# Second-product weight blocks read where they are summed, h2 kept in halves, and one group's order written out on two engines

## The chip, the cores and the metric

The kernel runs on one core of one Trainium2 chip. The metric is the device time of one execution in microseconds (us), as a median over runs. The profile is of one execution and has a time of its own.

## The reference

One encoder layer on 512 tokens of width 1024 in float32: a mixer with three branches (convolution, attention, spatial gating), then a feed-forward part. The change touches the feed-forward part alone:

```
h = rms_norm(x, norm_ffn_pre[l])                                   # 512 x 1024
f = jnp.square(jax.nn.relu(h @ w_ffn_up[l])) @ w_ffn_down[l]       # 1024 -> 4096 -> 1024
x = x + rms_norm(f, norm_ffn_post[l])
```

## The kernel before, in words

**Number format.** Every operand of a matrix product is cut into a high part (a copy on ACT into fp32r, `w_hi`, `h2h`) and a low part (original minus high on DVE, `w_lo`, `h2l`), and a product is three matmuls: high x high, high x low, low x high. So before PE can use a weight block of 128x1024, ACT makes one pass over it and DVE another behind it, and DVE's pass is needed by the third matmul.

**First product (h @ w_ffn_up).** The normalised `h`, transposed, lies in `h2h` and `h2l` (8 blocks of 128 rows of the contraction, times 512 tokens). The first four of the 32 column tiles are made plainly (`early`, `PLAIN`, one run for each half of the tokens). The other 28 come in seven groups `q = 1..7` of four tiles. A group is a 2x2 block product done with seven products instead of eight (`product(o, q, i, ...)`, i = 0..6), each of 24 matmuls of 256 columns. Its weight operands are the blocks `11`, `12`, `22`, the running sum `w_sum` (after 2, 3 and 4 additions) and `21 + 11`: `operand(q, i)` makes sum, high and low part. Its other operands are quarters of `h2` (products 0, 1 and 4) or four signed sums T[0..3] of the quarters (products 2, 3, 5, 6). These sums are the same for all groups and are made once, in `side()` and `parts()`, in the tiles `f` (scratch) and `ring`, at the start of group 1. Products 0 and 1 read the first and the second half of the contraction for the first 256 tokens, product 4 the second half for the others. The first half of `h2` is thus read last by product 0 of group 7, the second half by product 4 of group 7. Results leave through `snap` (a copy on ACT), `plus` (an addition on DVE) and `f_out` (two passes on ACT).

**Second product (f @ w_ffn_down).** The first half of the contraction is again done with seven block products p1, p5, p6, p2, p7, p4, p3 of four steps each (12 matmuls of 512 columns a step), the second half plainly in 16 steps (1, i) and (2, i) (24 matmuls a step), in the order of `seq`: p1 x4, (1,0), (1,1), p5 x2, (1,2), p5 x2, (1,3), p6 x2, (1,4), and so on. With B11, B12, B21, B22 the four blocks of the weights, p1 wants B11, p5 wants t1 = B11 + B12, p6 wants t1 + B22, p7 wants t3 = B22 + B12. Each of t1 and t3 comes in four pieces of 128x1024: a plain transfer from SP's queue brings B11 (or B22), and a transfer from POOL's queue with `accum_op=ALU.add` adds B12 to it in place. The pieces of t1 lie where `h2h` was and those of t3 where `h2l` was (same tags `hh`, `hl`). B11 for p1 and B22 for p6 are loaded a second time, like all other blocks, through three buffers `raw` (`top_up`). `prep(n + 2)` at step n makes the low and high parts of step n + 2 and of the moving operand of step n + 3.

**What sets the order.** TensorE's order is the program's (`keep_in_program_order`). On ACT, DVE, SP and POOL a scheduler places instructions when the kernel is built, by its own estimate of times; each engine then runs its row in order, and an instruction that waits holds everything behind it. A new tile in a tag waits until all readers of the old tile are done, as one whole.

Of the kernel before, what the change touches and what calls it, by code (L numbers as in the profile page):

```python
# [16 lines left out]
P = 128  # L17
# [31 lines left out]
def encoder_layer(ctx: ExitStack, tc: tile.TileContext, a: dict, out: bass.AP):  # L49
# [201 lines left out]
    def k_of(t):  # L251
        return t.rearrange("p (k s) -> p k s", s=S)

    hh = k_of(held("hh", "hh", F32R))
    hl = k_of(held("hl", "hl", F32R))
    with mk("p0") as p0:
# [512 lines left out]


    h2h = k_of(held("h2h", "hh", F32R, SHIFT))
    h2l = k_of(held("h2l", "hl", F32R, SHIFT))
    with mk("p4") as p4:
# [67 lines left out]
    def snap(src, t=None):  # L841
        if t is None:
            t = fp.tile([P, S], F32, tag="sn", bufs=4, name="snap")
        act.activation(t, src, AF.Copy)
        return t
# [5 lines left out]
    ring = fp.tile([P, 8 * 1024 + P], F32R, tag="ring", name="ring")  # L851

    def half(j, at):
        return ring[:, at + j * 1024:at + (j + 1) * 1024]

    def f_out(n, ts, src, sign):

        act.activation(src, src, AF.Relu, scale=sign)
        act.activation(f[:, n:n + 2, ts], src.rearrange("p (x t) -> p x t", x=2), AF.Square)


    for n in range(PLAIN):
        b = eb[n]
        run(unit_gen(b[:, 256:512], early[n], h2, slice(256, 512)))
        r = fp.tile([P, S], F32, tag="r", bufs=2, name="r")
        act.activation(r, b, AF.Relu)
        act.activation(f[:, n], r, AF.Square)

# [22 lines left out]
    def block(j, k):  # L891
        h_, l_ = quarter(j, (t1, t2)[k])
        vec.tensor_tensor(q4(B[j, k]), f32(h_), f32(l_), op=ALU.add)

    def parts(i):
        hi, lo = half(2 * i, SHIFT), half(2 * i + 1, SHIFT)
        act.activation(hi, sums[4 + i], AF.Copy)  # L897
        vec.tensor_tensor(lo, sums[4 + i], f32(hi), op=ALU.subtract)
        T[i] = q4(hi), q4(lo)

    def side():

        block(0, 0)
        block(0, 1)
        vec.tensor_tensor(sums[4], B[0, 0], B[0, 1], op=ALU.subtract)
        block(1, 1)
        vec.scalar_tensor_tensor(sums[5], sums[4], -1.0, B[1, 1], op0=ALU.mult, op1=ALU.subtract)
        block(1, 0)
        vec.scalar_tensor_tensor(sums[6], sums[5], -1.0, B[1, 0], op0=ALU.mult, op1=ALU.subtract)
        vec.tensor_tensor(sums[7], B[1, 1], B[0, 1], op=ALU.subtract)  # L910

    def operand(q, i):

        if q >= FT // 4:
            return
        g = lambda n: blocks[q, n]
        if i == 2:
            blocks[q, "x"] = wp.tile([P, 1024], F32, tag="raw", bufs=3, name="w_sum")
            vec.tensor_tensor(g("x"), g("21"), g("22"), op=ALU.add)
        if i == 3:  # L920
            vec.tensor_tensor(g("x"), g("x"), g("11"), op=ALU.add)
        if i == 4:
            vec.tensor_tensor(g("x"), g("x"), g("12"), op=ALU.add)
        if i == 6:
            vec.tensor_tensor(g("21"), g("21"), g("11"), op=ALU.add)
        raw = g(("11", "12", "x", "x", "x", "22", "21")[i])
        hi = wp.tile([P, 1024], F32R, tag="hi", bufs=3, name="w_hi")
        lo = wp.tile([P, 1024], F32R, tag="lo", bufs=3, name="w_lo")
        act.activation(hi, raw, AF.Copy)  # L929
        vec.tensor_tensor(lo, raw, f32(hi), op=ALU.subtract)  # L930
        blocks[q, i] = [t.rearrange("p (k c) -> p k c", c=256) for t in (hi, lo)]

    def product(o, q, i, m, first):
# [8 lines left out]
    def plus(ps_, t):  # L942
        r = fp.tile([P, S], F32, tag="r", bufs=2, name="r")
        vec.tensor_tensor(r, ps_, t, op=ALU.add)
        return r
# [18 lines left out]
    for p_ in ("p4", "p3"):  # L964
        for i in range(4):
# [20 lines left out]
    raws = []  # L986
    state2 = {}

# [5 lines left out]

    def load_t1():

        for n, tag in (("t1", "hh"), ("t3", "hl")):
            t = held(n, tag, F32)
            state2[n] = [t[:, i * 1024:(i + 1) * 1024] for i in range(4)]
# [38 lines left out]
    def w_prep(step):  # L1038
        p_, i = step
        top_up()  # L1040
        mine = [raws.pop(0) for _ in w_raws(step)]
        if p_ in ("p5", "p6", "p4"):
            src = state2["t1"][i]
            if mine:
                vec.tensor_tensor(src, src, mine[0], op=ALU.add)
        else:
            src = state2["t3"][i] if p_ == "p7" else mine[0]
        hi = wp.tile([P, 1024], F32R, tag="hi", bufs=3, name="w_hi")
        lo = wp.tile([P, 1024], F32R, tag="lo", bufs=3, name="w_lo")
        act.activation(hi, src, AF.Copy)  # L1050
        vec.tensor_tensor(lo, src, f32(hi), op=ALU.subtract)  # L1051
        wparts[step] = [t.rearrange("p (k c) -> p k c", c=512) for t in (hi, lo)]
        top_up()

    def prep(n):

        if n == 0:
            f_prep(seq[0])
        if n + 1 < len(seq):
            f_prep(seq[n + 1])  # L1060
        if n < len(seq):
            w_prep(seq[n])
        for m, at in (("t1", 0), ("t3", 8)):
            if at <= n < at + 4:
                load_sum(m, n - at)

    side()
    operand(1, 0)
    parts(0)
    operand(1, 1)  # L1070
    for q in range(1, FT // 4):
        c1, c2 = 4 * q, 4 * q + 2
        def ahead(i):
            if i + 2 < 7:
                operand(q, i + 2)
# [4 lines left out]
            if q == 1 and i in (0, 2, 3):  # L1080
                parts({0: 1, 2: 2, 3: 3}[i])

        ahead(0)
        ba = bank("a")
        product(ba, q, 0, quarter(0, t1), True)
        s1 = snap(ba)
        ahead(1)
        bd = bank("b")
        product(bd, q, 1, quarter(1, t1), True)
        f_out(c1, t1, plus(bd, s1), 1.0)  # L1090
# [5 lines left out]
        se = snap(be)  # L1096
        ahead(3)
        product(ba, q, 3, T[1], False)
        sv = snap(ba)
        load_block(q + 1, "22")  # L1100
# [7 lines left out]
        f_out(c1, t2, plus(be, sv), 1.0)  # L1108
        ahead(5)
# [38 lines left out]
    def finish(nh, t, xs=None):  # L1148
# [7 lines left out]
        act.activation(jk, src, AF.Square, accum_out=ss[:, t, nh:nh + 1])  # L1156
        vec.tensor_tensor(us[:, t, hf], src, gpo[:, hf], op=ALU.mult)
        if nh == 0:
# [85 lines left out]
```

## Time and profile before

| | us |
|---|---|
| median of 3 runs (1073.16 to 1078.03) | 1076.43 |
| profiled execution, its own time | 1074.35 |
| its span in the profile | 1072.6 |
| around the span | 1.75 |

The profile lists for each engine how long it was busy, in 40 slices how fast TensorE's clock was (9 is full), and the chain of work that ended last. A row of the timeline reads: start, duration, engine, line, operation, what is written from what, how many, and in brackets how long the engine had been idle and what released it. Starts are counted from the span's beginning.

### The profile page before, as it was taken

The page shows a single profiled execution, that of the slowest core. Times are in us where ns is not written, and L with a number is a line of the kernel's source. Part 1 is how long each engine was busy: PE and PEld are TensorE (multiplying, and loading weights), DVE is VectorE, ACT ScalarE, POOL GpSimd, SP SyncE. Part 2 cuts the span into 40 slices and gives each one's busy share as a digit, 9 for nine tenths or more (in the row PEclk, how much of TensorE's full clock was granted, in tenths as well). Part 3 has the DMA queues.
Part 4 walks back from the last instruction along what each step waited for, and adds up shares of the span by engine and source line. Part 5 has one row for each costly group of instructions (what it writes and reads, how often), then busy time and mean ns, then how long its engine had stood idle before and what let it go on. Part 6 is the DMA issues. An engine that isn't in the chain of part 4 may idle for free.

```text
span 1072.6 us, 14742 instructions
## 1 busy us (share of the span) xinstructions
PE 1049.0 (98%) x5688; PEld 903.6 (84%) x5688; DVE 827.0 (77%) x1296; ACT 579.9 (54%) x902; POOL 23.7 (2%) x40
## 2 busy tenths in 40 slices
PE   8999999999999999999999999999999998899997
PEld 7989898988878888888888888889899997688885
DVE  6696878978997797998898455478888787667746
ACT  5456677776664742344222673354677775455641
POOL 3000000000000000000000000000000002100000
PEclk9999999999999999999999999999999999999999
DMA  7342332233233333322333233645334219834432
GB/s 223 83 137 61 97 96 82 79 84 94 79 99 98 99 101 97 97 79 82 95 98 98 79 88 100 232 130 172 104 99 135 84 60 274 236 97 139 164 130 79
DMA packets 140550, 122.35 MB, mean 114 GB/s; under 512 B 4277, under 2 KB 116961, under 8 KB 140480
## 3 DMA queue, kind: packets, MB, share of 16 engines
q1 hardware_dynamic: 135296, 108.02, 32.8%
q0 software_dynamic: 4464, 11.82, 4.4%
q10 hardware_dynamic: 720, 1.57, 0.4%
q8 instruction: 44, 0.72, 0.3%
q14 instruction: 26, 0.21, 0.1%
HBM read 113.01 MB, written 4.19 MB: 109 GB/s over the span
## 4 chain that ended last, share of the span: by engine, by line
PE 87%; DVE 5%; DMA 4%; ACT 3%; issue 1%; SPq 0%; DVEq 0%; ACTq 0%
PE ps_a L58 66%; PE ps_b L58 18%; PE ps_b L62 3%; DMA w_raw<-in_w_ffn_down_dram 3%; DMA w_raw<-in_w_in_dram 1%; DVE us L1164 0%; DVE w_lo L1051 0%; ACT y L738 0%; ACT ring L897 0%; DVE jk L814 0%; DVE w_lo L151 0%; PE ps_a L62 0%; ACT jk L812 0%; SPq L274 0%; ACT w_hi L150 0%
## 5 line engine op out<-in xcount | busy, mean ns | idle before, releaser
L150 ACT ACTIVATE w_hi<-w_raw 128x1024 fp32r<-128x1024 f32 x116 | 122.8, 1059 | 214.2 <-PE ps_a L58 177.1
L58 PE MATMUL ps_a<-hh,w_hi 128*128 128x512 f32 (+1 forms) x536 | 205.4, 385 | 0.0
L58 PE MATMUL ps_a<-hh,w_lo 128*128 128x512 f32 (+1 forms) x536 | 202.9, 381 | 0.0
L58 PE MATMUL ps_a<-hl,w_hi 128*128 128x512 f32 (+1 forms) x536 | 202.5, 380 | 0.0
L359 DVE SCALAR_TENSOR_TENSOR acc<-apad,convw,acc 128x512 f32<-128x512 f32 x232 | 173.7, 749 | 5.0
L151 DVE TENSOR_TENSOR w_lo<-w_raw,w_hi 128x1024 fp32r<-128x1024 f32 x116 | 141.6, 1221 | 41.5 <-ACT w_hi L150 41.2
L58 PEld LDWEIGHTS ps_a<-hh,w_lo 128*128 128x128 f32 x536 | 100.3, 188 | 19.6
L58 PEld LDWEIGHTS ps_a<-hh,w_hi 128*128 128x128 f32 x536 | 100.5, 188 | 18.3
L58 PEld LDWEIGHTS ps_a<-hl,w_hi 128*128 128x128 f32 x536 | 100.5, 188 | 18.3
L58 PE MATMUL ps_a<-ring,w_hi 128*128 128x256 f32 x336 | 59.6, 281 | 0.1
L58 PEld LDWEIGHTS ps_a<-ring,w_hi 128*128 128x128 f32 x336 | 51.9, 192 | 0.3 <-ACT w_hi L929 0.3
L58 PE MATMUL ps_a<-w_hi,hh 128*128 128x256 f32 (+1 forms) x160 | 49.7, 311 | 0.0
L58 PE MATMUL ps_a<-ring,w_lo 128*128 128x256 f32 x168 | 47.4, 282 | 2.2 <-DVE w_lo L930 2.2
L58 PE MATMUL ps_a<-h2h,w_hi 128*128 128x256 f32 x176 | 48.9, 278 | 0.0
L58 PE MATMUL ps_a<-h2l,w_hi 128*128 128x256 f32 x176 | 48.8, 277 | 0.0
L58 PE MATMUL ps_a<-h2h,w_lo 128*128 128x256 f32 x176 | 48.7, 277 | 0.0
L58 PE MATMUL ps_a<-w_hi,hl 128*128 128x256 f32 (+1 forms) x160 | 48.7, 304 | 0.0
L58 PE MATMUL ps_a<-w_lo,hh 128*128 128x256 f32 (+1 forms) x160 | 48.6, 304 | 0.0
L494 ACT ACTIVATE e<-ps_b,m 128x512 f32<-128x512 f32 x64 | 43.4, 682 | 7.3 <-DVE m L490 7.1
L1051 DVE TENSOR_TENSOR w_lo<-w_raw,w_hi 128x1024 fp32r<-128x1024 f32 x28 | 34.2, 1221 | 16.4 <-ACT w_hi L1050 16.4
L58 PE MATMUL ps_a<-w_hi,ring 128*128 128x512 f32 x144 | 45.4, 389 | 0.0
L490 DVE CUSTOM_DVE_ANT_0 ps_b<-ps_b,al 128x512 f32<-128x512 f32 x64 | 43.5, 699 | 0.6 <-PE ps_b L58 0.2
(306 smaller groups left out, 2438.4 us busy)
## 6 DMA issues: line engine op xcount, KB each, us to landing
w_raw<-in_w_in_dram SPq DMA_DIRECT2D x80, 512.0 KB, 3.7
w_raw<-in_w_ffn_down_dram SPq DMA_DIRECT2D x36, 512.0 KB, 4.1
w_raw<-in_w_ffn_up_dram SPq DMA_DIRECT2D x32, 512.0 KB, 4.7
w_raw<-in_w_proj_attn_dram SPq DMA_DIRECT2D x8, 512.0 KB, 3.9
w_raw<-in_w_proj_sgu_dram SPq DMA_DIRECT2D x8, 512.0 KB, 4.0
w_raw<-in_w_proj_conv_dram SPq DMA_DIRECT2D x8, 512.0 KB, 4.0
w_raw<-in_w_out_dram SPq DMA_DIRECT2D x8, 512.0 KB, 3.6
t<-in_w_ffn_down_dram SPq DMA_DIRECT2D x8, 512.0 KB, 11.0
```

The source lines that it names most:

```text
L58: return tc.keep_in_program_order(nc.tensor.matmul(*args, **kw))
L62: return tc.keep_in_program_order(nc.tensor.transpose(*args, **kw))
L150: act.activation(hi, raw, AF.Copy)
L151: vec.tensor_tensor(lo, raw, f32(hi[:, :]), op=ALU.subtract)
L359: vec.scalar_tensor_tensor(o, apad[:, c, j:j + S], convw[:, c, j:j + 1], acc, op0=ALU.mult, op1=ALU.add)
L490: vec.tensor_tensor_reduce(b, b, nal[:, 384 - q * P:896 - q * P], 1.0, 3.0e38, ALU.add, ALU.min, m)
L494: act.activation(e, b, AF.Exp, bias=m, scale=-1.0, accum_out=l)
L1051: vec.tensor_tensor(lo, src, f32(hi), op=ALU.subtract)
```

## The change

1. `h2h` and `h2l` become two tiles each, one for each half of the contraction (`held` gives a pair, `KOf` picks the half). The tags are `hha`, `hhb`, `hla`, `hlb`.
2. The plain transfers for t1 and t3 stand apart from the adding ones (`load_sum`, `add_sum`). The program issues the first two pieces of t1 after product 0 of group 7, the others after product 4. The adding transfers are issued in `prep` of p1 (for t1) and of p6 (for t3).
3. p1 takes its B11 from the piece of t1 before the addition, and p6 its B22 from the piece of t3 before the addition. The eight loads of these blocks into `raw` go.
4. In group 1, and in the four plain tiles ahead of it, the order on ACT and DVE is written out by hand and kept (`order`, `pin`): `plain`, `side`, `side_hi`, `side_lo`, `w_sum`, `w_hi`, `w_lo`, `first`. The pin ends with `pin[0] = False` after product 4 of group 1.
5. `us` and `xs` at the end become pairs of tiles too, and `xs` is loaded in two transfers.

```diff
-    def held(name, tag, dt, at=0):
-        return hp.tile([P, KT * S + P], dt, tag=tag, name=name)[:, at:at + KT * S]
+    def held(name, tag, dt, at=(0, 16)):
+
+        return [hp.tile([P, KT // 2 * S + n], dt, tag=tag + h_, name=name)[:, o:o + KT // 2 * S]
+                for h_, n, o in zip("ab", (112, 16), at)]
...
+    def order(i):
+
+        return tc.keep_in_program_order(i) if pin[0] else i
...
-    B_OF = {"p1": [(1, 1)], "p2": [(2, 1)], "p3": [(2, 2)], "p4": [(2, 1)], "p5": [], "p6": [(2, 2)],
-            "p7": []}
+    B_OF = {"p1": [], "p2": [(2, 1)], "p3": [(2, 2)], "p4": [(2, 1)], "p5": [], "p6": [], "p7": []}
...
     def load_sum(n, i):
-        t = state2[n][i].rearrange("p (k c) -> p k c", c=512)
-        k, c = (2 * i, 0) if n == "t1" else (8 + 2 * i, 512)
-        nc.sync.dma_start(t, rows("w_ffn_down", k, c))
-        pool.dma_start(t, rows("w_ffn_down", 2 * i, 512), accum_op=ALU.add)
+
+        if i % 2 == 0:
+            sums2[n, i // 2] = hp.tile([P, KT // 2 * S + (16 if i else 112)], F32,
+                                       tag=("hh" if n == "t1" else "hl") + "ab"[i // 2], name=n)
+        nc.sync.dma_start(sum_at(n, i).rearrange("p (k c) -> p k c", c=512),
+                          rows("w_ffn_down", *((2 * i, 0) if n == "t1" else (8 + 2 * i, 512))))
+
+    def add_sum(n, i):
+
+        pool.dma_start(sum_at(n, i).rearrange("p (k c) -> p k c", c=512), rows("w_ffn_down", 2 * i, 512),
+                       accum_op=ALU.add)
...
-        if p_ in ("p5", "p6", "p4"):
-            src = state2["t1"][i]
-            if mine:
-                vec.tensor_tensor(src, src, mine[0], op=ALU.add)
+        if p_ in ("p1", "p5", "p6", "p4"):
+            src = sum_at("t1", i)
+            if p_ in ("p6", "p4"):
+                vec.tensor_tensor(src, src, mine[0] if mine else sum_at("t3", i), op=ALU.add)
...
-        for m, at in (("t1", 0), ("t3", 8)):
-            if at <= n < at + 4:
-                load_sum(m, n - at)
-
-    side()
-    operand(1, 0)
-    parts(0)
-    operand(1, 1)
+        if n < len(seq) and seq[n][0] in ("p1", "p6"):
+            add_sum("t1" if seq[n][0] == "p1" else "t3", seq[n][1])
+
+
+    block(0, 0)
+    block(0, 1)
+    side(0)
...
+    def first(i):
+
+        if i == 0:
+            w_hi(1, 3)
+            w_lo(1, 3)
+            side_hi(2)
+            w_sum(1, 4)
...
+        elif i == 4:
+            w_lo(1, 6)
+            pin[0] = False
...
         product(ba, q, 0, quarter(0, t1), True)
+        if q == FT // 4 - 1:
+            for i in range(2):
+                load_sum("t1", i)
...
         if q == FT // 4 - 1:
-            top_up()
-            load_t1()
+            for n, i in (("t1", 2), ("t1", 3), ("t3", 0), ("t3", 1), ("t3", 2), ("t3", 3)):
+                if i == 0:
+                    top_up()
+                load_sum(n, i)
```

**DVE in group 1.** This is DVE's row from the low part of product 2's weights to the low part of product 3's (each `w_lo` is the low part of the next product's weights; `ring` is a low part of one of T[0..3], `w_sum` an addition into the running sum, `w_raw<-w_raw` the sum 21 + 11 for product 6, `r<-ps_b` is `plus`). Before:

```order
L930 TENSOR_TENSOR w_lo_6923<-w_sum_6920,w_hi_6922 128x1024
L944 TENSOR_TENSOR r_6985<-ps_b_6960,snap_6953 128x512
L921 TENSOR_TENSOR w_sum_6920<-w_sum_6920,w_raw_6783 128x1024
L898 TENSOR_TENSOR ring_6793<-f_6782,ring_6793 128x1024
L925 TENSOR_TENSOR w_raw_6785<-w_raw_6785,w_raw_6783 128x1024
L930 TENSOR_TENSOR w_lo_6957<-w_sum_6920,w_hi_6956 128x1024
```

And of the change, on to the low part for product 4 (`w_lo_6991`):

```order
L951 TENSOR_TENSOR w_lo_6925<-w_sum_6897,w_hi_6924 128x1024
L939 TENSOR_TENSOR w_sum_6897<-w_sum_6897,w_raw_6787 128x1024
L951 TENSOR_TENSOR w_lo_6960<-w_sum_6897,w_hi_6959 128x1024
L939 TENSOR_TENSOR w_sum_6897<-w_sum_6897,w_raw_6793 128x1024
L970 TENSOR_TENSOR r_6993<-ps_b_6965,snap_6957 128x512
L930 TENSOR_TENSOR ring_6797<-f_6786,ring_6797 128x1024
L951 TENSOR_TENSOR w_lo_6991<-w_sum_6897,w_hi_6990 128x1024
```

One pass instead of four stands between the low parts for products 2 and 3; the others moved behind.

**DVE in group 2.** The place is ahead of the low part for product 4 of group 2 (`w_lo_7232` before, `w_lo_7236` in the change), from the `plus` of product 1 on. `w_sum_7400` and `w_sum_7404` are the next group's running sum, `w_raw_7237` and `w_raw_7241` the next group's 21 + 11. Before:

```order
L944 TENSOR_TENSOR r_7226<-ps_b_7201,snap_7194 128x512
L923 TENSOR_TENSOR w_sum_7163<-w_sum_7163,w_raw_7061 128x1024
L919 TENSOR_TENSOR w_sum_7400<-w_raw_7237,w_raw_7296 128x1024
L930 TENSOR_TENSOR w_lo_7232<-w_sum_7163,w_hi_7231 128x1024
L925 TENSOR_TENSOR w_raw_7237<-w_raw_7237,w_raw_7235 128x1024
```

And of the change (`w_lo_7202` is the low part for product 3):

```order
L941 TENSOR_TENSOR w_raw_6999<-w_raw_6999,w_raw_6997 128x1024
L939 TENSOR_TENSOR w_sum_7167<-w_sum_7167,w_raw_6997 128x1024
L970 TENSOR_TENSOR r_7230<-ps_b_7205,snap_7198 128x512
L951 TENSOR_TENSOR w_lo_7202<-w_sum_7167,w_hi_7201 128x1024
L939 TENSOR_TENSOR w_sum_7167<-w_sum_7167,w_raw_7069 128x1024
L937 TENSOR_TENSOR w_sum_7404<-w_raw_7241,w_raw_7300 128x1024
L941 TENSOR_TENSOR w_raw_7241<-w_raw_7241,w_raw_7239 128x1024
L951 TENSOR_TENSOR w_lo_7236<-w_sum_7167,w_hi_7235 128x1024
```

The low part for product 3 moved behind the `plus`, and the next group's 21 + 11 moved ahead of the low part for product 4.

**SP's queue at the start of the second product.** `w_raw` are loads through the three buffers, t1 and t3 the plain transfers of the sums. Before:

```order
L992 DMA w_raw_8506<-in_w_ffn_down_dram 128x2x512
L992 DMA w_raw_8508<-in_w_ffn_down_dram 128x2x512
L992 DMA w_raw_8510<-in_w_ffn_down_dram 128x2x512
L1004 DMA t3_8513<-in_w_ffn_down_dram 128x2x512
L1004 DMA t1_8512<-in_w_ffn_down_dram 128x2x512
L992 DMA w_raw_8528<-in_w_ffn_down_dram 128x2x512
L1004 DMA t1_8512<-in_w_ffn_down_dram 128x2x512
L992 DMA w_raw_8565<-in_w_ffn_down_dram 128x2x512
L1004 DMA t1_8512<-in_w_ffn_down_dram 128x2x512
L992 DMA w_raw_8614<-in_w_ffn_down_dram 128x2x512
```

And of the change (t1_8383 and t3_8522 lie in the first halves, t1_8513 and t3_8525 in the second):

```order
L1016 DMA w_raw_8516<-in_w_ffn_down_dram 128x2x512
L1031 DMA t3_8522<-in_w_ffn_down_dram 128x2x512
L1031 DMA t1_8383<-in_w_ffn_down_dram 128x2x512 x2
L1031 DMA t3_8522<-in_w_ffn_down_dram 128x2x512
L1016 DMA w_raw_8518<-in_w_ffn_down_dram 128x2x512
L1016 DMA w_raw_8520<-in_w_ffn_down_dram 128x2x512
L1031 DMA t3_8525<-in_w_ffn_down_dram 128x2x512
L1031 DMA t1_8513<-in_w_ffn_down_dram 128x2x512 x2
L1031 DMA t3_8525<-in_w_ffn_down_dram 128x2x512
L1016 DMA w_raw_8660<-in_w_ffn_down_dram 128x2x512
```

Four transfers for the sums moved ahead of the second load through the buffers, and all eight now stand ahead of the fourth; the three first loads were B11 for p1 and are now the weights of (1,0), (1,1) and (1,2).

## Rows read from the trace of the kernel before

**Rows 1.** The page: busy time, share of the span and instructions of each engine; then the shares of the chain that ended last.

```profile
PE 1049.0 (98%) x5688; PEld 903.6 (84%) x5688; DVE 827.0 (77%) x1296; ACT 579.9 (54%) x902; POOL 23.7 (2%) x40
PE 87%; DVE 5%; DMA 4%; ACT 3%; issue 1%; SPq 0%; DVEq 0%; ACTq 0%
```

**Rows 2.** Waits of PE between 738 and 1066 us: who was waited for, total us, times, longest us.

```profile
PE ps_b L58 <- DVE w_lo L1051: 4.6, 3, 2.6
PE ps_a L58 <- DVE w_lo L930: 2.2, 2, 1.8
PE ps_a L58 <- ACT snap L844: 1.4, 1, 1.4
PE ps_b L58 <- ACT w_hi L1050: 1.4, 1, 1.4
```

**Rows 3.** Timeline of PE in group 1: the first matmul of product 1, the two that waited in products 2 and 3, the first of product 5.

```profile
754.71 0.28 PE L58 MATMUL ps_b<-h2h,w_hi 128*128 128x256 f32 x1
...
758.30 0.39 PE L58 MATMUL ps_a<-ring,w_lo 128*128 128x256 f32 x1 [0.49 <-DVE w_lo L930]
...
763.44 0.51 PE L58 MATMUL ps_a<-ring,w_lo 128*128 128x256 f32 x1 [1.75 <-DVE w_lo L930]
...
770.38 0.28 PE L58 MATMUL ps_b<-ring,w_hi 128*128 128x256 f32 x1
```

**Rows 4.** The chain that ended last, in order of time: product 1 of group 2 (start, us, what).

```profile
778.70 2.72 PE ps_b L58 x24
```

**Rows 5.** Stretches: us, busy time (and instructions) of PE, PEld, DVE, ACT, POOL, granted TensorE clock as a share of full, DMA share, GB/s.

```profile
763.40:767.00 3.60, 3.56 (x17) 3.56 (x18) 3.54 (x4) 2.00 (x2) 0.00 (x0) 0.53 0.44 145
788.00:885.00 97.00, 97.00 (x858) 97.00 (x858) 80.22 (x78) 72.67 (x101) 0.00 (x0) 1.00 0.31 98
885.00:930.00 45.00, 37.62 (x171) 30.20 (x170) 30.45 (x29) 22.71 (x28) 9.56 (x8) 0.92 1.01 274
...
924.00:927.00 3.00, 3.00 (x9) 2.32 (x8) 1.28 (x2) 0.00 (x0) 0.96 (x1) 0.50 1.12 229
```

**Rows 6.** Timeline of DVE in group 1: the first sums of `h2`, the first addition into `w_sum` (21 + 22), then everything from the low part of product 2's weights to that of product 3's.

```profile
739.97 3.49 DVE L893 TENSOR_TENSOR f<-h2h,h2l 128x1024 f32<-128x1024 f32 x3
...
752.46 1.22 DVE L919 TENSOR_TENSOR w_sum<-w_raw 128x1024 f32<-128x1024 f32 x1
...
757.02 1.23 DVE L930 TENSOR_TENSOR w_lo<-w_sum,w_hi 128x1024 fp32r<-128x1024 f32 x1 [1.08 <-ACT w_hi L929]
758.16 0.68 DVE L944 TENSOR_TENSOR r<-ps_b,snap 128x512 f32<-128x512 f32 x1
758.77 1.22 DVE L921 TENSOR_TENSOR w_sum<-w_sum,w_raw 128x1024 f32<-128x1024 f32 x1
759.90 1.22 DVE L898 TENSOR_TENSOR ring<-f,ring 128x1024 fp32r<-128x1024 f32 x1
761.03 1.22 DVE L925 TENSOR_TENSOR w_raw<-w_raw 128x1024 f32<-128x1024 f32 x1
762.17 1.22 DVE L930 TENSOR_TENSOR w_lo<-w_sum,w_hi 128x1024 fp32r<-128x1024 f32 x1
```

**Rows 7.** Timeline of ACT in group 1: the first pass on the first plain tile, and the high part of product 2's weights.

```profile
744.02 0.60 ACT L866 ACTIVATE r<-ps_a 128x512 f32<-128x512 f32 x1 [4.80 <-PE ps_a L58]
...
755.92 1.06 ACT L929 ACTIVATE w_hi<-w_sum 128x1024 fp32r<-128x1024 f32 x1
```

**Rows 8.** Timeline of PE in the second product: its first matmul, two that waited, and its last.

```profile
890.06 0.39 PE L58 MATMUL ps_a<-w_hi,ring 128*128 128x512 f32 x1
...
903.74 0.79 PE L58 MATMUL ps_b<-w_lo,f_part 128*128 128x512 f32 x1 [0.75 <-DVE w_lo L1051]
...
923.41 0.50 PE L58 MATMUL ps_b<-w_lo,ring 128*128 128x512 f32 x1 [2.62 <-DVE w_lo L1051]
...
1064.95 0.39 PE L58 MATMUL ps_a<-w_hi,f_part 128*128 128x512 f32 x1
```

**Rows 9.** The chain that ended last, in order of time: one step on which PE gets no rest, and the longest piece that is not PE's (from issue to landing).

```profile
893.90 12.87 DMA w_raw<-in_w_ffn_down_dram
...
1021.82 8.16 PE ps_b L58 x36
```

**Rows 10.** Issues at the start of the second product: SP's queue (L992 is a load through the buffers, L1004 a plain transfer of a sum, here t3's first piece), POOL's first adding transfer (which waits for that piece's landing); then the time from issue to landing of the transfers of the sums.

```profile
862.51 0.37 SPq L992 DMA_DIRECT2D w_raw<-in_w_ffn_down_dram  x1
...
881.59 0.37 SPq L992 DMA_DIRECT2D w_raw<-in_w_ffn_down_dram  x1
884.70 0.37 SPq L1004 DMA_DIRECT2D t<-in_w_ffn_down_dram  x1
...
889.08 1.22 POOL L1005 DMA_DIRECT2D t<-in_w_ffn_down_dram  x1 [150.59 <-DMA t<-in_w_ffn_down_dram]
...
DMA to landing us min/median/max: 3.8/9.9/13.7
```

**Rows 11.** DMA queues between 855 and 1000 us: packets, MB, share of the 16 engines' time. q1 is SP's, q0 POOL's (the eight adding transfers).

```profile
q1 hardware_dynamic: 9520, 18.35, 36.9%
q0 software_dynamic: 2176, 4.19, 15.9%
```

**Rows 12.** Timeline of DVE and ACT at the start of the second product: low part of p1's first weight block, high parts of its third and fourth.

```profile
886.92 1.22 DVE L1051 TENSOR_TENSOR w_lo<-w_raw,w_hi 128x1024 fp32r<-128x1024 f32 x1
...
891.40 1.04 ACT L1050 ACTIVATE w_hi<-w_raw 128x1024 fp32r<-128x1024 f32 x1
...
894.43 1.05 ACT L1050 ACTIVATE w_hi<-w_raw 128x1024 fp32r<-128x1024 f32 x1
```

More of the change, by code (lines that the diff above doesn't have):

```diff
@@ L843, in snap @@
             t = fp.tile([P, S], F32, tag="sn", bufs=4, name="snap")
-        act.activation(t, src, AF.Copy)
+        order(act.activation(t, src, AF.Copy))
         return t
@@ L892, in block, with side, side_hi, side_lo @@
         h_, l_ = quarter(j, (t1, t2)[k])
[L893 to L915, printed above, removed]
+        order(vec.tensor_tensor(q4(B[j, k]), f32(h_), f32(l_), op=ALU.add))
+    def side(i):
+        if i in (0, 3):
+            m, n = ((0, 0), (0, 1)) if i == 0 else ((1, 1), (0, 1))
+            order(vec.tensor_tensor(sums[4 + i], B[m], B[n], op=ALU.subtract))
+        else:
+            order(vec.scalar_tensor_tensor(sums[4 + i], sums[3 + i], -1.0, B[1, 2 - i], op0=ALU.mult,
+                                           op1=ALU.subtract))
+    def side_hi(i):
+        T[i] = q4(half(2 * i, SHIFT)), q4(half(2 * i + 1, SHIFT))
+        order(act.activation(half(2 * i, SHIFT), sums[4 + i], AF.Copy))
+    def side_lo(i):
+        order(vec.tensor_tensor(half(2 * i + 1, SHIFT), sums[4 + i], f32(half(2 * i, SHIFT)), op=ALU.subtract))
+    def w_sum(q, i):
         g = lambda n: blocks[q, n]
@@ L918, in operand, with w_hi, w_lo @@
             blocks[q, "x"] = wp.tile([P, 1024], F32, tag="raw", bufs=3, name="w_sum")
[L919 to L926, printed above, removed]
+            order(vec.tensor_tensor(g("x"), g("21"), g("22"), op=ALU.add))
+        elif i in (3, 4):
+            order(vec.tensor_tensor(g("x"), g("x"), g("11" if i == 3 else "12"), op=ALU.add))
+        elif i == 6:
+            order(vec.tensor_tensor(g("21"), g("21"), g("11"), op=ALU.add))
+    def w_hi(q, i):
         hi = wp.tile([P, 1024], F32R, tag="hi", bufs=3, name="w_hi")
         lo = wp.tile([P, 1024], F32R, tag="lo", bufs=3, name="w_lo")
-        act.activation(hi, raw, AF.Copy)
-        vec.tensor_tensor(lo, raw, f32(hi), op=ALU.subtract)
+        blocks[q, i] = hi, lo, blocks[q, ("11", "12", "x", "x", "x", "22", "21")[i]]
+        order(act.activation(hi, blocks[q, i][2], AF.Copy))
+    def w_lo(q, i):
+        hi, lo, raw = blocks[q, i]
+        order(vec.tensor_tensor(lo, raw, f32(hi[:, :]), op=ALU.subtract))
         blocks[q, i] = [t.rearrange("p (k c) -> p k c", c=256) for t in (hi, lo)]
+    def operand(q, i):
+        w_sum(q, i)
+        w_hi(q, i)
+        w_lo(q, i)
     def product(o, q, i, m, first):
@@ L1062, in prep @@
             w_prep(seq[n])
-        for m, at in (("t1", 0), ("t3", 8)):
-            if at <= n < at + 4:
-                load_sum(m, n - at)
-    side()
-    operand(1, 0)
-    parts(0)
-    operand(1, 1)
+        if n < len(seq) and seq[n][0] in ("p1", "p6"):
[3 more added lines that the diff above has]
+    side(0)
+    block(1, 1)
+    side(1)
+    block(1, 0)
+    plain(0)
+    plain_out(0)
+    side_hi(0)
+    side_lo(0)
+    plain(1)
+    w_hi(1, 0)
+    plain_out(1)
+    w_lo(1, 0)
+    side(2)
+    plain(2)
+    w_hi(1, 1)
+    plain_out(2)
+    side_hi(1)
+    w_lo(1, 1)
+    w_sum(1, 2)
+    side_lo(1)
+    plain(3)
+    w_hi(1, 2)
+    plain_out(3)
+    w_lo(1, 2)
+    w_sum(1, 3)
+    def first(i):
[4 more added lines that the diff above has]
+            w_sum(1, 4)
+        elif i == 1:
+            w_hi(1, 4)
+        elif i == 2:
+            side_lo(2)
+            w_lo(1, 4)
+            side(3)
+            w_hi(1, 5)
+            w_lo(1, 5)
+            w_sum(1, 6)
+            side_hi(3)
+            side_lo(3)
+        elif i == 3:
+            w_hi(1, 6)
+        elif i == 4:
+            w_lo(1, 6)
+            pin[0] = False
     for q in range(1, FT // 4):
@@ L1079, in ahead, with behind @@
                 prep(i - 5)
-            if q == 1 and i in (0, 2, 3):
-                parts({0: 1, 2: 2, 3: 3}[i])
+        def behind(i):
+            if q == 1:
+                first(i)
         ahead(0)
@@ L1089, in encoder_layer @@
         product(bd, q, 1, quarter(1, t1), True)
+        behind(1)
         f_out(c1, t1, plus(bd, s1), 1.0)
@@ L1096, in encoder_layer @@
         se = snap(be)
+        behind(2)
         ahead(3)
@@ L1099, in encoder_layer @@
         sv = snap(ba)
+        behind(3)
         load_block(q + 1, "22")
```

63 lines of the change are left out of this document (38 added, 25 removed).

## The prediction

> **What bounds the kernel now.** The first view is the page. PE is busy 98% of the span and holds 87% of the chain that ended last; what is left on that chain is DVE 5%, DMA 4%, ACT 3% [rows 1]. So PE is the bound, and an edit gains only where PE stops or runs slowly and something else ends that. The second view is the list of PE's waits over the part that the change touches: low parts of weights, L930 in the first product and L1051 in the second, and one `snap` and one `w_hi` beside them [rows 2]. A wait understates its cost, so I measured each place against PE's own pace.
>
> *Group 1.* Without rest a product takes 2.72 us [rows 4]. Product 1 starts at 754.71, so product 5 is due at 754.71 + 4 x 2.72 = 765.59; it starts at 770.38 [rows 3]. Loss: 4.8 us. Two waits of 0.49 and 1.75 for L930 lie in it [rows 3], and behind the second the granted clock is 0.53 for 3.60 us (between the chip's levels of 2.4 and 1.2 GHz) [rows 5], which is 3.60 x 0.47 = 1.7 us more. DVE shows why: after the low part for product 2 it does `plus`, an addition into `w_sum`, a `ring` pass and 21 + 11, and only at 762.17 the low part for product 3 [rows 6], which ends at 763.39. Product 3 was due at 754.71 + 2 x 2.72 = 760.15, its third matmul 0.23 later.
>
> *Start of the second product.* Its 720 matmuls (28 steps of 12, 16 of 24) at 8.16 / 36 = 0.227 us [rows 9] take 163.2 us. From 890.06 the end is due at 1053.3; the last starts at 1064.95 [rows 8] and ends 0.23 later. Loss: 11.9 us. The waits are at 903.74 and 923.41 [rows 8]; behind them the chain holds a load of 12.87 us [rows 9], and the DMA share from 885 to 930 is 1.01 [rows 5]. Clock 0.50 from 924 to 927 [rows 5] is part of the loss. So here the transfers are the limit: from 788 to 885 the share was 0.31 with the clock at 1.00 [rows 5].
>
> **The change, part by part.**
>
> *Transfers.* SP's queue moved 18.35 MB in 36.9% of 145 us, 35 loads of 524 KB: 145 x 0.369 / 35 = 1.53 us of all 16 engines each. The eight adding transfers took 15.9%: 2.88 us each [rows 11]. Eight loads go. Four plain transfers move ahead: they wait for the first half of `h2` alone, free after product 0 of group 7, four products before the second half. The second half comes free where t3's first piece is issued now, at 884.70 [rows 10], so the first at 884.7 - 4 x 2.72 = 873.8, where the share is 0.31. From 885 to 930 go four plain transfers and p1's fourth block (7.7 us) and as many of p6's four loads (6.1) as fall there: 45 x 1.01 = 45.5 us of transfers become 32 to 38, and the queue is no longer full. The three loads issued up to 881.59 [rows 10] were p1's and are now those of (1,0), (1,1), (1,2).
>
> *What is late next there.* (a) t1's second half, behind t3's third piece on SP. That piece would land like today's first, 884.70 to 889.08 [rows 10]; each next 1.53 later: t1's third at 890.6, fourth at 892.1. ACT makes the high parts of p1's third and fourth block at 891.40 and 894.43 today [rows 12]. No stall. (b) The adding transfers. The first may start after p1's first low part, 886.92 + 1.22 = 888.1 [rows 12]. With the longest landing of 13.7 [rows 10] it is in at 902. p5 begins after four p1 steps and two plain ones, at 890.06 + 10.9 + 10.9 = 911.8, its copies (1.05 + 1.22) at 909.5. Spare: 7 us. (c) Of t3, the addition comes after p6's DVE pass and p7 wants it only after the four steps of p2 and two plain ones at least, 21.8 us: hidden. I take the whole 11.9; the low end is 7.8 (third rival).
>
> *The pinned order.* I walk DVE's new row from its first pass, 739.97, with 1.14 from pass to pass, 1.22 to the end of one, 0.61 for a `plus` [rows 6], 1.25 where a pass needs the one before it, and 1.06 for ACT's `w_hi` [rows 7]. First, eleven passes: three of `block` and `side` up to s1 at 744.74, then 745.88 block, 747.01 low of T0, 748.14 low for product 0, 749.28 s2, 750.41 low for 1, 751.55 first `w_sum`, 752.68 low of T1. Then low for 2 at 753.88, ends 755.10 (due 757.65, the third matmul); `w_sum` 755.13; `w_hi` to 757.43; low for 3 to 758.68 (due 760.37, 1.7 spare where 3.0 was lacking); `w_sum` 758.71; `plus`; T2's low; low for 4 to 762.80 (due 763.09); s3; low for 5 to 765.07 (due 765.81); 21 + 11; T3's low; `plus`; low for 6 to 769.07 (due 768.53): 0.5 to 0.6 late. So of 4.8 in group 1 about 0.6 stays.
>
> *Behind the pin.* The scheduler's row for group 2 is another: 21 + 11 of the next group stands ahead of the low part for product 4, and the low part for 3 behind `plus`. From 769.07 the same walk gives: low for 3 at 778.2 to 779.4 (due 780.0), then three additions at 779.4, 780.6 and 781.8, then low for 4 at 783.0 to 784.2. Group 2 starts at 771.6, product 4's third matmul is due at 771.6 + 4 x 2.72 + 0.23 = 782.7: 1.5 late. Left: 0.6 + 1.5 = 2.1; gain 4.8 - 2.1 = 2.7. Bounds: 4.8 if neither is late, 0 by the fourth rival.
>
> *Nothing for the rest.* The halves read the same elements with the same instructions. The order of groups 3 to 7 is as before. `xs` in two transfers adds one on POOL, busy 2% [rows 1].
>
> **Sum.** 11.9 + 2.7 = 14.6, bounds 7.8 and 16.7. All of it lies inside the span of 1072.6, and the 1.75 around it stays, so the profiled execution's 1074.35 gives 1059.75. The median of the runs shown is 2.08 above it; I carry half of that: **1060.8**.
>
> **Rivals.** What can be told from no change in this kernel is 0.5%, 5.4 us: 1071.05 to 1081.8.
>
> 1. *DVE becomes the bound at the second product's start.* It is busy 30.45 of 45 us there, and its best share over a long stretch is 80.22 / 97 = 0.827 [rows 5]. The same work at that share takes 36.8 us; PE without stops wants 45 - 11.9 = 33.1. Then 3.7 less is gained: 1064.5. Against it, DVE's passes stand back to back in [rows 6], so the share can be higher.
>
> 2. *The halves come free no earlier* (the change doesn't do what it says): all transfers at 884.7. p1's blocks then land from 889 on, the first some 1 late against today's 890.06, the others by 4 to 5, and the clock falls once (1.7): some 6.8 less, 1067.6. Against it, product 0 of group 7 is the last reader of the first half.
>
> 3. *t1's last piece shares the engines with the first adding transfer.* If it lands as the load on the chain did, 12.87 [rows 9] after an issue at about 885.7, that is 898.6, with copies 900.9, against p1's fourth step's third matmul at 890.06 + 3 x 2.72 + 0.23 = 898.45: 2.4 late, and 1.7 of clock. 4.1 less: 1064.9. For it, the loads landed in 4.4 to 12.9 here [rows 9, 10]; against it, that was under a full queue. The Trainium skill, DMA: Bandwidth & Descriptors, section Queues, rings and completion order, says that a DMA engine takes turns between the queues it has work for, packet by packet, so an adding transfer issued later does push back a load already on its way. By that rule one adding transfer (2.88) would move the landing from 892.1 to 895.0 and cost nothing, two to 897.9 and cost 1.7 before the clock; a 12.87 beside two busy queues agrees with it.
>
> 4. *Group 1 gives back all.* The first addition into `w_sum` moves from 752.46 [rows 6] to 751.55. The trace shows no wait there, so block 22 may have landed any time before. If it lands at 752.46, all behind shifts by 0.9: low for 4 is 0.6 late, for 6 1.5 late, and the clock falls (1.7); with the 1.5 in group 2 nothing of the 4.8 is left: 1060.8 + 2.7 = 1063.5.
>
> 5. *Slower: the adding transfers of t1 run strictly one behind another, d us each.* The last lands at 889.4 + 4d, wanted for p5's fourth step at 923.1. At d = 13.7 [rows 10] that is 21.1 late, with three falls of the clock 26: 1087. It eats the gain from d = 10.8 and is slower by 0.5% from 12.4. Against it, each took 2.88 of the engines [rows 11].
>
> **How the numbers follow.** Forecast 0.58; rival 1 0.12; 2 0.04; 3 0.09; 4 0.08; 5 0.03; something that I don't see 0.06, of which 0.05 within 0.5% and 0.01 slower. Faster: 0.58 + 0.12 + 0.04 + 0.09 + 0.08 = 0.91; same 0.05; slower 0.04. The forecast's own range is 1058.5 to 1063. The bounds of the sum give 1057.6 to 1066.6 against the profiled execution; the runs of before spread by 3.3 below the median and 1.6 above it, so I take a part of that on both sides: 1056.5 to 1069, which holds rivals 1 to 4.
>
> **What would show it.** Four plain transfers on SP's queue near 874 (some 868 by a clock that starts earlier by group 1's gain), not 885. In group 1 no PE wait over 0.6 in products 2 and 3; in group 2 one of about 1.5 for the low part of product 4. From the second product's start no wait of ACT or DVE for a transfer up to p6, a DMA share well below 1, the clock at 1.00, and 163 us from PE's first matmul to its last. It would be wrong if a load there lands 10 us or more after its issue, if PE's waits move from DMA to DVE at the same size, or if the pinned row loses in group 2 more than it gains in group 1.

## The result, and the profile after

| | before | after |
|---|---|---|
| median, us | 1075.62 (4 runs, 1073.16 to 1078.03) | 1061.98 (4 runs, 1059.95 to 1064.41) |
| profiled execution, its own time | 1074.35 | 1059.99 |
| its span | 1072.6 | 1058.2 |

The ratio is 0.9874, with a 95% interval of 0.9838 to 0.9911: 13.6 us faster. The profiled execution became 14.4 us faster. (Of the kernel before there is one run more here than in the prediction, so its median is 1075.62 and not 1076.43.) The page of after, which answers to [rows 1]:

```profile
PE 1042.6 (99%) x5688; PEld 900.0 (85%) x5688; DVE 827.0 (78%) x1296; ACT 580.5 (55%) x902; POOL 24.3 (2%) x41
PE 91%; DVE 5%; ACT 2%; issue 1%; DMA 1%; DVEq 0%; ACTq 0%
```

PE's waits between 725 and 1060 us (engine, who was waited for: total us, times, longest), which answer to [rows 2], and the one that is left in group 2:

```profile
PE ps_a L58 <- DVE w_lo L951: 1.6, 2, 1.4
PE ps_b L62 <- DVE jk L827: 0.6, 1, 0.6
```

```profile
784.33 0.39 PE L58 MATMUL ps_a<-h2h,w_lo 128*128 128x256 f32 x1 [1.39 <-DVE w_lo L951]
```

DVE around it: product 3's low part, then three additions, then the low part that PE waits for (start, duration):

```profile
778.13 1.23 DVE L951 TENSOR_TENSOR w_lo<-w_sum,w_hi 128x1024 fp32r<-128x1024 f32 x1
779.39 1.23 DVE L939 TENSOR_TENSOR w_sum<-w_sum,w_raw 128x1024 f32<-128x1024 f32 x1
780.65 1.22 DVE L937 TENSOR_TENSOR w_sum<-w_raw 128x1024 f32<-128x1024 f32 x1
781.91 1.23 DVE L941 TENSOR_TENSOR w_raw<-w_raw 128x1024 f32<-128x1024 f32 x1
783.05 1.22 DVE L951 TENSOR_TENSOR w_lo<-w_sum,w_hi 128x1024 fp32r<-128x1024 f32 x1
```

All waits of the second product are gone. Its first and last matmul, and the stretch 887 to 927 us (columns as in [rows 5]):

```profile
887.59 0.39 PE L58 MATMUL ps_a<-w_hi,ring 128*128 128x512 f32 x1
...
1050.58 0.39 PE L58 MATMUL ps_a<-w_hi,f_part 128*128 128x512 f32 x1
```

```profile
887.00:927.00 40.00, 40.00 (x181) 33.24 (x180) 35.98 (x33) 24.45 (x29) 8.52 (x8) 1.00 0.84 180
```

1050.58 + 0.23 - 887.59 = 163.2 us, the time of 720 matmuls without a stop: of the 11.9 us that [rows 8] showed lost, all came back. The issues on SP's and POOL's queues, which answer to [rows 10]:

```profile
860.04 0.37 SPq L1016 DMA_DIRECT2D w_raw<-in_w_ffn_down_dram  x1
871.35 1.91 SPq L1031 DMA_DIRECT2D t<-in_w_ffn_down_dram  x4
876.68 2.80 SPq L1016 DMA_DIRECT2D w_raw<-in_w_ffn_down_dram  x2
882.23 2.85 SPq L1031 DMA_DIRECT2D t<-in_w_ffn_down_dram  x4
```

```profile
885.96 1.22 POOL L1036 DMA_DIRECT2D t<-in_w_ffn_down_dram  x1 [147.72 <-DVE w_lo L1083]
...
905.32 1.19 POOL L1036 DMA_DIRECT2D t<-in_w_ffn_down_dram  x1 [9.04 <-DVE t L1077]
```

The pieces in the first halves are loaded four products before those in the second. And the adding transfers now wait for DVE: t1's for p1's low part (L1083), t3's for p6's sum (L1077). Such a wait, which keeps a transfer from being issued, is called a hold below.

### The profile page after: what moved, and what is told of

Same layout as the page of the kernel before. It is cut to its first block, busy times and chain, and to the rows that moved or that the text cites. A ratio compares the mean times of both kernels' runs of the same rounds, so it can differ in the third digit from the quotient of the medians.

```text
span 1058.2 us, 14724 instructions
## 1 busy us (share of the span) xinstructions
PE 1042.6 (99%) x5688; PEld 900.0 (85%) x5688; DVE 827.0 (78%) x1296; ACT 580.5 (55%) x902; POOL 24.3 (2%) x41
## 3 DMA queue, kind: packets, MB, share of 16 engines
HBM read 108.81 MB, written 4.19 MB: 107 GB/s over the span
## 4 chain that ended last, share of the span: by engine, by line
PE 91%; DVE 5%; ACT 2%; issue 1%; DMA 1%; DVEq 0%; ACTq 0%
PE ps_a L58 69%; PE ps_b L58 19%; PE ps_b L62 3%; DVE w_lo L951 1%; DMA xx<-in_x_dram 1%; DVE us L1257 0%; DVE w_lo L151 0%; ACT y L751 0%; DVE hs L303 0%; DVE jk L827 0%; PE ps_a L62 0%; DVE hl L224 0%; ACT jk L825 0%; DVE jk L1247 0%; DVE rs_s L206 0%
```

## The experiments

Each loss "in the second product" below is the time from its first to the end of its last matmul, less 163.2 us: 11.9 before, 0.0 after. It is read from the one profiled execution of each run. The edits are shown in part, with `...` for what is left out.

### The two parts alone

```diff
 e_no_pin: group 1 as in the kernel before
-    pin = [True]
+    pin = [False]
...
+    side()
+    operand(1, 0)
+    parts(0)
+    operand(1, 1)
...
 e_pin_only: the kernel before, with order(), first() and behind() of the change
```

> The change without its written order: group 1 and the four plain tiles are coded as before, the halves, the shared blocks and the moved transfers stay. Theory A (two separate gains that add: about 2.4 us in the first product, 11.9 us from the second product's start): group 1 loses its 4.8 us again, group 2 loses nothing, the second product still runs without a stop in 163.2 us. Span 1058.2 + 2.4 = 1060.6, time about 1064.4. Rival B (the order also shifted the second product's transfers, so that its gain is worth less alone): PE waits for w_lo or w_hi come back after the second product's start and the span is 1063 or more.

Measured: 1062.22 (ratio 0.9868, 0.9835 to 0.9901), span 1060.3, 0.0 lost in the second product. Its waits of PE are those of before in group 1:

```profile
PE ps_a L58 <- DVE w_lo L948: 2.2, 2, 1.8
```

So the second product's gain needs nothing from the order, and between the two profiled executions the order is worth 2.1 us of the span. The medians do not show it: the ratio to before is 0.9868 without the order, 0.9874 with it, and 0.9841 when the change was run again (below). Three of the change's eight runs were 4 us slower than the others (last section), which hides a gain of 2.

> The kernel before with the written order of group 1 alone; h2, the transfers and p1's and p6's blocks as before. Theory A: group 1 loses about 0.9 and group 2 about 1.6 instead of 4.8 and 0, the 11.9 us at the second product's start stay: span 1072.6 - 2.4 = 1070.2, time about 1073.3. Rival B: the order gives nothing by itself (0.0, span 1072.6), since a later stop eats it.

Measured: 1075.54 against 1077.21 (ratio 0.9977, 0.9959 to 0.9995), span 1074.1. The second product begins 2.4 us earlier, as expected, but loses 15.9 instead of 11.9 in this execution:

```profile
PE ps_b L58 <- DVE w_lo L1064: 4.6, 2, 3.8
PE ps_a L58 <- ACT snap L844: 3.8, 1, 3.8
PE ps_a L58 <- DVE w_lo L938: 1.6, 2, 1.4
PE ps_b L58 <- ACT w_hi L1063: 1.2, 1, 1.2
```

The timed runs bear the 2.4 us out (1.7 between the medians), the profiled one gives them back in the full stretch, as rival B said. Which holds alone stays open. With the stretch free, the order is worth 2.1 us in the profiled execution.

### What made the stretch free

```diff
 e_whole_h2: one tile each for h2h and h2l; all pieces after product 4
 e_loads_back
-    B_OF = {"p1": [], ... "p6": [], "p7": []}
+    B_OF = {"p1": [(1, 1)], ... "p6": [(2, 2)], "p7": []}
...
 e_p1_loads: p1's four only; e_p6_loads_back: p6's four only
```

> The change with h2h and h2l as one tile each again: the pieces of t1 and t3 can only be loaded when product 4 of group 7 is done; p1 and p6 still read their blocks where the sums are made, the eight loads stay away, the written order stays. Theory A (the halves are needed): p1's four blocks are issued at about 882 instead of 871, the first lands about 4.4 us later, so p1 starts some 1 us late and its other blocks come 4 to 5 late, with one fall of the clock some 6.8 us: span 1065.0, time about 1068.8. Rival C (the eight missing loads are the whole gain): span 1058.2 to 1059, time 1062 to 1063.

Measured: 1066.18 (ratio 0.9892), span 1065.2. That looks like theory A's 1065.0, but the trace says otherwise. PE waits 0.4 for p1's first high part and 0.9 for its low part, and not again:

```profile
PE ps_a L58 <- DVE w_lo L952: 1.8, 2, 1.4
PE ps_a L58 <- DVE w_lo L1083: 0.9, 1, 0.9
PE ps_b L62 <- DVE jk L828: 0.4, 1, 0.4
PE ps_a L58 <- ACT w_hi L1082: 0.4, 1, 0.4
```

The second product loses 1.4, and the product ahead of it ends 0.6 late: these 2 us are what the trace shows of the halves. Of the other 5.0 us of the span, 1.0 lies ahead of group 1 (its product 0 starts at 752.79 instead of 751.74), and 4.0 are a slower pace of PE behind the wait in group 2 (last section): 8.48 us for three products instead of 8.16, as here on the chain:

```profile
858.91 8.48 PE ps_a L58 x72
```

So the number of theory A came, but not for its reason. Whether the halves have to do with the slower pace was not tested: all four runs lie between 1065.8 and 1067.0, none of them 4 us lower.

> The change with p1's and p6's blocks loaded a second time through the three buffers, as before; halves, early pieces and the written order stay. Rival C (the missing loads are the gain): the 11.9 us come back nearly whole, span about 1068 to 1070. Rival D (taking four transfers out of the full stretch is the gain): nothing comes back, span 1058 to 1059. Theory A (both): 12.2 us of transfers are back but four plain ones stay early, 45.5 - 6.1 = 39 us in 45; the weights of (1,0) are issued only when p1's first low part frees a buffer, near 886, and land 4.4 to 12.9 later: between 0 and 5.5 late, with a fall of the clock; I take 4: span 1062, time about 1066.

Measured: 1074.35 (ratio 0.9974, 0.9958 to 0.999), span 1070.8, 12.6 lost in the second product. Theory A's 4 was far too small, and rival D, which expected no loss, is out: four transfers issued early gained nothing while the loads were there. Rival C's size came. The long piece on the chain is a load again, and POOL shows what stands beside it, the first and the fourth adding transfer:

```profile
893.01 17.95 DMA w_raw<-in_w_ffn_down_dram
```

```profile
875.56 1.22 POOL L1036 DMA_DIRECT2D t<-in_w_ffn_down_dram  x1 [137.36 <-DVE r L970]
...
880.42 1.19 POOL L1036 DMA_DIRECT2D t<-in_w_ffn_down_dram  x1 [0.34 <-issue]
```

p1 no longer reads the pieces of t1, nor p6 those of t3, so nothing holds an adding transfer but the landing of the plain one. Four of them have been issued by 880.42; in after the first goes at 885.96. Two causes are mixed here, the eight loads and the two lost holds. The next runs take them apart for p1 and p6 one by one; all eight loads with both holds were not run.

> The change with p6's four blocks loaded a second time again; p1 reads from t1 as in the change. t3's adding transfers then stand right behind t1's, near 896 to 900 instead of 905 to 921. Theory A: the queue is past its peak there and p5, p6 wait for none of it: span 1058.2 to 1060. Theory F: t3's adding transfers delay the weights of (1,2) and p6 as t1's did for (1,0): 2 us or more, span 1060 to 1064.

Measured: 1068.85 (ratio 0.9915), span 1067.1, 8.6 lost in the second product, though p6's four loads come only after 900. That is theory F's direction at more than its price. t3's adding transfers, freed, stand ahead of t1's on POOL:

```profile
875.86 1.22 POOL L1036 DMA_DIRECT2D t<-in_w_ffn_down_dram  x1 [137.66 <-DVE r L970]
879.81 1.20 POOL L1036 DMA_DIRECT2D t<-in_w_ffn_down_dram  x1 [2.73 <-DMA t<-in_w_ffn_down_dram]
```

and t1's third piece, a plain transfer issued at 882.78, takes 11 us where it took 5.4 in after (the four there took 4.6 to 7.9); later p6's first load, behind three adding transfers, takes 10.4:

```profile
882.78 11.06 DMA t<-in_w_ffn_down_dram
...
904.21 10.41 DMA w_raw<-in_w_ffn_down_dram
```

The first costs 3.1 us at p1. The second costs 4.8: DVE stands for 6 us at p6's first sum, and a low part that p5 needs stands behind it in DVE's row.

```profile
914.71 1.23 DVE L1077 TENSOR_TENSOR t<-t,w_raw 128x1024 f32<-128x1024 f32 x1 [5.99 <-DMA w_raw<-in_w_ffn_down_dram]
```

The DMA share from 885 to 930 (last column but one) does not tell this run from after, which had 0.80 there and lost nothing:

```profile
885.00:930.00 45.00, 39.08 (x175) 31.47 (x174) 33.11 (x31) 22.63 (x28) 7.23 (x6) 0.96 0.79 193
```

```diff
 e_p6_held: p6's four loads are there, t3's additions wait for p6 as in the change
...
+                if p_ == "p6":
+                    vec.tensor_tensor(src[:, 960:], src[:, 960:], b[:, 960:], op=ALU.add)
+                    src, b = src[:, :960], sum_at("t3", i)[:, :960]
```

> As the run with p6's loads back, but p6's sum takes 960 of its 1024 columns from the piece of t3 and the rest from the loaded block (the same numbers, one more short DVE instruction a step), so that t3's adding transfers wait for p6 as in the change; the four loads are there. Theory F (the loss of 8.6 us in the second product came from t3's adding transfers, which went out at 876 and 880 ahead of t1's second half): PE loses 0 to 2 us from the second product's start, span 1058.2 to 1060.5 (4.2 more at the slower pace). Theory G (it is the four loads themselves): 6 us or more lost in the second product.

Measured: 1060.81 (ratio 0.9846), span 1059.0, 0.1 lost in the second product. POOL's first issue is at 886.39 and t3's first at 908.05:

```profile
886.39 1.22 POOL L1036 DMA_DIRECT2D t<-in_w_ffn_down_dram  x1 [147.88 <-DVE w_lo L1088]
...
908.05 1.19 POOL L1036 DMA_DIRECT2D t<-in_w_ffn_down_dram  x1 [10.23 <-DVE t L1081]
```

The same four loads cost 8.6 without the hold and 0.1 with it. So for p6 the bytes alone cost next to nothing, and what t3's hold saves is 8.5 us when these loads are there. What its loss would cost with no load of p6's own to be delayed was not run; 3.1 of the 8.6 fell on t1's third piece, which the change has too.

> The change with p1's four blocks loaded a second time again; p6 keeps reading from t3. The adding transfers of t1 then wait only for their plain pieces, not for p1's low parts. Theory F (with the loads the adding transfers start near 879 and fill the queue before the weights come, so four loads and the lost hold cost as much as eight): the loss of the run with all eight loads, 12.4 us, comes back whole or nearly, span 1069 to 1071. Theory G (each load costs its share of the transfers): half of it, span about 1064.

Measured: 1065.62 (ratio 0.9885), span 1064.3, 1.8 lost in the second product; 4.0 of the span are the slower pace. Neither theory: the freed additions go out at 880.24, ahead of p1's start at 891.61, and p1's loads lose little.

```diff
 e_p1_held: p1's high part from the load, its low part from the piece of t1
+        if p_ == "p1":
+            src = sum_at("t1", i)
```

> As the run with p1's loads back, but p1's low part subtracts from the piece of t1 (the same numbers), so that each adding transfer waits for p1's low part as in the change; the four loads are there. Theory F (it is the time of the adding transfers): the queue stays free until 886, the fourth block and the weights of (1,0) come 5 to 9 us after their issue at 885.7 and 889, in time or up to 1.6 late, at most one fall of the clock: span 1058.2 to 1061.5. Theory G (it is the four loads and the buffers that they hold): the same as without the hold, 1064 to 1071.

Measured: 1065.96 (ratio 0.9897), span 1062.1, 3.6 lost in the second product. Here holding t1's additions does not help: the four loads cost 2 to 4 us either way, with a load of 12 us on the chain, issued at 890.05:

```profile
890.05 12.03 DMA w_raw<-in_w_ffn_down_dram
```

So theory F holds for p6 and falls for p1, where the loads themselves (theory G, at a smaller price) count. Without holds, p1's four loads cost 1.8 and p6's four 8.6, 10.4 together, against 12.6 for all eight; where the other 2.2 come from was not traced.

### The disputed price

```diff
 e_late_t1: t1's second half from POOL's queue, behind the first adding transfer (order kept)
-            for n, i in (("t1", 2), ("t1", 3), ("t3", 0), ...
+            for n, i in (("t3", 0), ...
...
+        if n == 0:
+            load_sum("t1", 2)
+            load_sum("t1", 3)
```

> The change with the plain transfers of t1's third and fourth piece issued from POOL's queue, behind the first adding transfer, near 887.2 and 888.4 instead of 882.5 to 883: the disputed price of a plain transfer that shares the engines with an adding one. By the landings of the change (4.6 to 8 us) they are in at 892 to 896, with high and low part (2.3) 0.8 to 3.5 after p1's third step is due at 893.3; I take 2.5 and one fall of the clock (1.7): span 1062. Rival 3 of the prediction (12.9 us as on the chain of before): 900 + 2.3, 9 late and two falls of the clock: span 1069 or more.

Measured: 1069.34 (ratio 0.9919), span 1068.1, of which 4.0 are the slower pace, so 1064.1 without it; 5.9 lost in the second product. The piece lands 9.2 us after its issue:

```profile
889.90 9.16 DMA t<-in_w_ffn_down_dram
```

That lies between the two prices (4.6 to 8, and 12.9). The Trainium skill, DMA: Bandwidth & Descriptors, section Queues, rings and completion order, has a DMA engine take turns between queues, packet by packet; this run puts plain and adding transfers on one queue, so it does not show that rule, but the 11.06 us of the run above, with plain and adding transfers on two queues, agrees with it.

### The written order, mended

```diff
 e_both_lows: group 1: side(3) ahead of w_lo(1, 3), w_sum(1, 6) ahead of w_lo(1, 4)
+            order(... 21 + 11 ..., q in (2, 3))          # behind w_lo(2, 4)
+            order(... 21 + 22 ..., q == 3)               # behind w_lo(2, 4)
 e_lows_2: without the last line
```

> The change with the written order mended at its two late low parts: in group 1 the sum for product 6 and T3 are made earlier, in group 2 the low part for product 4 stands ahead of the next groups' sums. Theory A: the two stops of PE (0.3 and 1.6 us) go, nothing else changes: span 1058.2 - 1.9 - 0.3 = 1056.0. Theory H (what the spread of the runs is: after a stop PE goes on either at 2.72 us a product or at 2.83, until its next stop, and 38 products at 0.11 more are 4.2 us): without a stop between group 1 and the second product every run has one pace, and the times no longer fall into two groups 4.2 us apart; median about 1057.8. Rival I (the two groups of times come from something else): the two groups stay, at 1057.8 and 1062.

Measured: 1061.01 (1060.89 to 1061.46, ratio 0.984), span 1059.7. Both stops went, but group 3 got three, of 0.6 to 0.8:

```profile
797.16 0.38 PE L58 MATMUL ps_a<-ring,w_lo 128*128 128x256 f32 x1 [0.76 <-DVE w_lo L951]
800.77 0.38 PE L58 MATMUL ps_a<-ring,w_lo 128*128 128x256 f32 x1 [0.60 <-DVE w_lo L951]
804.43 0.39 PE L58 MATMUL ps_a<-h2h,w_lo 128*128 128x256 f32 x1 [0.65 <-DVE w_lo L951]
```

An addition that is kept back in one group makes the next one late. As PE still stopped, theory H was not put to its test; the times lie in one group all the same.

> The change itself once more, beside the mended order on the same chip: times in two groups, near 1060 and near 1064 (theory H and rival I alike); if its profiled execution is of the upper group, a span of about 1062.4, products of 2.83 us behind the stop in group 2, clock 1.00 (theory H), or a stop or a lower clock somewhere else (rival I).

Measured: 1060.15, 1060.19, 1060.23 and 1064.11, ratio 0.9841; the profiled execution was of the lower group (span 1058.4), so it did not decide.

> As the mended order, but the next group's running sum for product 2 goes back to its place ahead of group 2's low part for product 4 (moving it too made group 3's low parts late by 0.6 to 0.8 three times); only the sums 21 + 11 of groups 2 and 3 stand behind it. By the walk of the written order the low part for product 4 then ends near 781.1, due 781.9: no stop in groups 1 to 3. Theory A: span 1058.4 less 0.5, 1.6 and 0.3 of slow pace, 1056.0, lower runs at 1057.8. Theory H: with no stop between the start of group 1 and the second product all five times within 1 us of each other. Rival I: one or two of five times 4.2 higher.

Measured: 1061.78 (ratio 0.9873), span 1056.8: one stop of 0.3 is left, in group 3.

```profile
PE ps_a L58 <- DVE w_lo L951: 0.3, 1, 0.3
```

The profiled execution is the fastest of all (1058.52), but the other three are at 1061.62 to 1062.47. With a stop left, this decides between theory H and rival I no more than the runs before. No median beats the change's clearly.

## Why the prediction was right

The forecast was 1060.8 and the measured median is 1061.98; the profiled execution was forecast at 1059.75 and took 1059.99.

- *Second product, 11.9.* Gained: 11.9. The pieces were issued at 871.35 (forecast 874, or 868 with an earlier clock), and from 885 to 930 the two queues took 80% of 45 us, 36 us (forecast 32 to 38), and no transfer there took more than 8.1 us to land:

```profile
q0 software_dynamic: 2176, 4.19, 56.9%
q1 hardware_dynamic: 1969, 3.77, 22.8%
```

- *Groups 1 and 2, gain 2.7 with 0.6 and 1.5 left.* From product 1 at 754.46 the 48 products to 887.59 are due after 130.6 us and took 133.1: 2.6 left, gain 2.2. The wait in group 2 was forecast at 1.5 and is 1.39, at the instruction that was named; its low part was walked to 783.0 and started at 783.05. The one in group 1 was forecast at 0.5 to 0.6 and is 0.16. Missing in the walk: some 0.7 us of slower pace between 762 and 769, which made PE later and that wait shorter. That group 1 comes out near its 0.6 is in part luck.
- *The median.* I carried half of the 2.08 between median and profiled execution. The runs fall into two groups of two (below), so the median is the middle between them, and that it lies near the forecast is luck.
- *The reason, only half right.* That transfers make PE stop at the second product's start, and that the stops end with fewer and earlier ones, is what the trace shows: with the eight loads back 12.6 us are lost again. But the sum took each load at its 1.53 us and asked whether the queue was full, and the runs do not follow that measure. p6's four loads cost 0.1 with t3's hold and 8.6 without it, at a share of 0.79 against 0.80 in after. The prediction saw that t3's additions come behind p6's DVE pass, and took this only as a reason why they are hidden; that the same wait keeps them out of the way of other transfers was put at nothing. For t1's additions, which it had behind p1's first low part, no gain of the hold is shown (1.8 lost without it, 3.6 with it).
- *The rivals.* The DVE bound did not come: 35.98 busy of 40, with PE busy throughout. The late halves were priced at 6.8 and cost 2, the slower pace apart: all pieces after the first landed in time. The shared load was priced by 12.9 and took 9.2 and 11.1 where it was provoked. Group 1 did not give back all: its first addition into `w_sum` started at 751.35 without a wait, and 0.9 of the loss is left there. t1's adding transfers landed 2.5 to 3.3 us apart, far from the 10.8 at which the gain would have gone, and p5 did not wait for them.

## What to carry to other kernels

A transfer that is not needed soon can be held by a wait on something that comes late, else it goes out as soon as it can and may delay those that are needed at once. When data is used where it lies, ask which wait that adds, and try it: beside p6's loads t3's wait was worth 8.5 us, beside p1's loads t1's was worth nothing. The share of a stretch in which the queues are busy did not tell here whether a needed load was late. A walk of one engine's row with a few durations from the trace forecast one wait to 0.1 us and another to 0.4; an order written out by hand must be walked past its end, into the rows that the scheduler then makes.

## What the runs showed of the hardware

**Two paces of PE after a stop.** In some executions PE goes on after a stop at 2.83 us for 24 matmuls instead of 2.72, until a later stop, with the granted clock at 1.00 and no wait. The chain of after, and of the run with p1's loads back, behind the same wait in group 2:

```profile
797.99 8.16 PE ps_a L58 x72
```

```profile
798.50 8.48 PE ps_a L58 x72
```

The stretch 785 to 885 us of both (matmuls in brackets behind PE's busy time, the granted clock in the last column but two): 885 against 851.

```profile
785.00:885.00 100.00, 100.00 (x885) 100.00 (x884) 82.57 (x81) 73.68 (x101) 0.00 (x0) 1.00 0.38 121
```

```profile
785.00:885.00 100.00, 100.00 (x851) 100.00 (x850) 79.46 (x78) 71.42 (x99) 2.42 (x2) 1.00 0.36 112
```

From the wait at 784.3 to the second product lie 38 products: 38 x 0.11 = 4.2 us. The change's times lie at 1059.95, 1059.99 and 1063.97, 1064.41, that is 4.0 to 4.5 apart, and again at 1060.2 and 1064.1. With the last wait at 801 (e_lows_2) 31 products, 3.4 us, would be at stake, and the times lie 3.1 to 4.0 apart. In e_both_lows all five lie within 0.6, though it stops too. Over these 38 products the slower pace was seen in three profiles (e_whole_h2, e_p1_loads, e_late_t1), each behind the wait in group 2. It also comes in short stretches: in group 1 of five profiles with the written order, the one of after among them, and in four products of group 2 in both runs with p6's loads. The profiles of before and e_no_pin show none in the seven groups. That it makes the upper times of the other runs fits their size but was not seen. What chooses the pace is open.

**An adding transfer is dear.** 4.19 MB through q0 took 56.9% of 45 us, 3.2 us of all engines for each of eight (2.88 from [rows 11]); a plain one of the same size took 1.4 there (22.8% of 45 us for 3.77 MB) and 1.53 in [rows 11].
